# AdaLN side work in a diffusion trunk: row sums by 32x32 transposes and one full-size product, and the vectors dealt anew to the FFN halves

## The chip, the cores and the metric

One core of a Trainium2 chip runs the whole program: TensorE (PE, matmul), VectorE (DVE), ScalarE (ACT), GpSimd (POOL), and SyncE (SP), which issues the DMA transfers. The metric is the device time of one execution in microseconds; the number that counts is the median of several executions.

## What is computed

Two layers of a diffusion backbone over 256 latent tokens and 256 context tokens of width 1024. Each layer is a half-step SwiGLU feed-forward (FFN), a token mixer (windowed attention, short convolution and global attention, merged by gates), and a second half-step FFN. Each sub-layer is normalised and modulated by vectors that come from the conditioning:

```
def _ada(cvec, w, b):
    m = jax.nn.silu(cvec) @ w + b                    # (1024) @ (1024, 9*1024)
    return [m[..., j, :, :] for j in range(N_MOD)]   # 9 vectors: shift, scale, gate, three times

m, mc = _ada(c, w_ada[i], b_ada[i]), _ada(c_ctx, w_ada[i], b_ada[i])
x  = x  + 0.5 * m[2]  * _swiglu(_modulate(x,  g, m[0],  m[1]),  wg, wu, wd)
xc = xc + 0.5 * mc[2] * _swiglu(_modulate(xc, g, mc[0], mc[1]), wg, wu, wd)
...                                                  # mixer with m[3], m[4], m[5]; FFN with m[6], m[7], m[8]
```

All is float32. The conditioning is two vectors (latent and context), so each of the 18 modulation "vectors" below means 1024 values for each of the two.

## The kernel before

Activations are held transposed, features on the 128 partitions and the 512 tokens (256 of each stream) along the free dimension. Every large product is made of float32r matmuls in three parts: a weight block and an activation are each split into a high part and a remainder (`wh`, `wl` and `hh`, `hl`), and `mm_chunk` (lines 202 to 214) issues three matmuls for each block of 128 rows: high by high (line 211), high by low (212), low by high (213). A chunk is eight such blocks, 24 matmuls; in the FFN's down projection six or five, 18 or 15. `split_w` (line 185) makes `wh` by a ScalarE copy (188) and `wl` by a VectorE subtraction (189); there are three buffers of each.

Modulation vectors 0 and 1 of layer 0 are made at the start of the program by TensorE. The other 16 are made as side work within three of the four FFN halves by the class `Side`. For each vector, a step loads 128 rows of `w_ada` (a tile `adar`, 128x1024, line 267) and VectorE multiplies it by a per-partition scalar and adds it into an accumulator `adac` of 128x2x1024, once for each of the two conditionings (lines 278 and 282). After eight steps the accumulator holds, on each partition, a partial sum; the sum over the 128 partitions is still missing. `rows` (line 289) takes it on TensorE: for each conditioning v and each j of 0 to 3 a product of a 128x32 matrix `pick` (ones in column v) with 256 columns of the accumulator, written to 32 partitions of a PSUM tile. These are eight fp32 products; the trace counts two matmuls for each, and all have line 298. `ada_done` then transposes the PSUM tile by 32x32 blocks on VectorE (242), adds the bias (244) and scales (249 or 255).

Where the side work stands is set by calls: `ffn` calls `side` once ahead of each chunk pair and each half of a down projection, and calls 4 to 33 carry one or two steps each:

```
h = ffn(i, 0, h, (0, 1), side(4, 34, 1, 2) if i else side(4, 34, 2), (i, 1), ...)
```

Seven vectors (2 to 8 of layer 0) go to the first FFN half, five (0 to 4 of layer 1) to the second of layer 0, four (5 to 8 of layer 1) to the first of layer 1. From this program order a list scheduler in the build sets each engine's order; the engines run theirs in order and wait on semaphores. At the end of an FFN half the `Queue` runs the next norm's steps (`norm`, `modulate`; line 360 is the variance, 394 and 196 make the next `hl`), and the mixer's first chunks are the keys (`keys`, line 526; `keys_rstd` with lines 539 to 548).

Of the kernel before, what the change touches and what calls it, by code (L numbers as in the profile page):

```python
# [60 lines left out]
def trunk(ctx, tc, x, c, ctxt, c_ctx, w_ada, b_ada, norm_g, ffn_w_gate, ffn_w_up, ffn_w_down,  # L61
# [77 lines left out]
    ident_b = const.tile([P, P], BF16, name="ident_b")  # L139
    mask_b = const.tile([P, 2, P], BF16, name="mask_b")  # L140
    sel = const.tile([P, 32], F32, name="sel")
    pick = const.tile([P, 2, 32], F32, name="pick")
    sink_t = const.tile([P, DEPTH, NH], F32, name="sink_t")
    nsink_t = const.tile([P, DEPTH, NH], F32, name="nsink_t")

# [8 lines left out]
    def make_rest():  # L154
        vl.append(transposed_rows(*vl_rows[1], "vl1"))
        nc.vector.tensor_copy(ident_b, ident)
        nc.vector.tensor_copy(mask_b, cst[:, MSK:MSK + 2 * P].rearrange("p (a b) -> p a b", a=2))

        nc.vector.memset(sel, 0.0)
        nc.vector.tensor_copy(sel[:, 0:2], blk2)  # L160

        nc.vector.memset(pick, 0.0)
        for v in range(2):
            nc.vector.memset(pick[:, v, v:v + 1], 1.0)
        nc.vector.tensor_scalar(out=nsink_t, in0=sink_t, scalar1=-1.0, scalar2=None, op0=ALU.mult)

    def b_ada_v(i, k0, n):
# [72 lines left out]
    def ada_done(i, a, ps, k0=0, n=KD):  # L240
        tt = small.tile([P, S], F32, tag="t1k", name="ada_t", bufs=2)
        nc.vector.transpose(out=tt[:, :32 * n], in_=ps[:, :32 * n])
        m = mods[i][:, KD * a + k0:KD * a + k0 + n, :]
        nc.vector.tensor_tensor(
            out=m, in0=tt[:, :32 * n].rearrange("p (m r) -> p m r", r=32)[:, :, 0:2],
            in1=b_ada_v(i, KD * a + k0, n).unsqueeze(2).to_broadcast([P, n, 2]), op=ALU.add,
        )
        if a % 3 == 1:
            nc.vector.scalar_tensor_tensor(
                out=m, in0=m, scalar=1.0,  # L250
                in1=norm_v(i, a // 3)[:, k0:k0 + n].unsqueeze(2).to_broadcast([P, n, 2]),
                op0=ALU.add, op1=ALU.mult,
            )
        elif a in (2, 8):
            nc.vector.tensor_scalar(out=m, in0=m, scalar1=0.5, scalar2=None, op0=ALU.mult)

    class Side:
        def __init__(self):  # L260
            self.todo, self.loaded, self.acc, self.full = [], [], None, None

        def load(self, pool):
            if self.todo:
                i, a, k = self.todo.pop(0)
                raw = pool.tile([P, D], F32, tag="adar", name="adar", bufs=2)
                nc.sync.dma_start(out=raw, in_=w_ada[i][k * P:(k + 1) * P, a * D:(a + 1) * D])
                self.loaded.append((i, a, k, raw))

        def add(self, pool):  # L270
            if not self.loaded:
                return
            i, a, k, raw = self.loaded.pop(0)
            if k == 0:
                self.acc = pool.tile([P, 2, D], F32, tag="adac", name="adac", bufs=1)
            for v in range(2):
                if k == 0:
                    nc.vector.tensor_scalar(
                        out=self.acc[:, v], in0=raw, scalar1=c32[:, k, v:v + 1], scalar2=None, op0=ALU.mult
                    )  # L280
                else:
                    nc.vector.scalar_tensor_tensor(  # L282
                        out=self.acc[:, v], in0=raw, scalar=c32[:, k, v:v + 1], in1=self.acc[:, v],
                        op0=ALU.mult, op1=ALU.add,
                    )
            if k == KD - 1:
                self.full = (i, a, self.acc)

        def rows(self):
            if self.full is None:  # L290
                return
            i, a, acc_t = self.full
            self.full = None
            ps = aux()
            for v in range(2):
                r4 = acc_t[:, v].rearrange("p (m j r) -> p j m r", j=4, r=32)
                for j in range(4):
                    nc.tensor.matmul(
                        ps[32 * j:32 * j + 32, :S], pick[:, v], r4[:, j], start=(v == 0), stop=(v == 1)
                    )  # L300
            ada_done(i, a, ps)

        def step(self, pool, n):
            for _ in range(n):
                self.rows()
                self.add(pool)
                self.load(pool)

        def flush(self, pool):
            while self.loaded or self.full:  # L310
                self.rows()
                self.add(pool)

    ada_side = Side()

# [122 lines left out]
    def ffn(i, f, h, streams, side, tail, first=None):  # L438
        x = parts_of(h)
        with tc.tile_pool(name="ffn", bufs=1) as fp:  # L440
            for f0, fn in ((0, 12), (12, 10)):
                g = [fp.tile([P, 12, T], F32R, tag=t, name=t) for t in ("gh", "gl")]
                for fb in range(0, fn, 2):
                    c0 = (f0 + fb) * P
                    given = f0 + fb == 0 and first is not None
                    if not given:
                        raws = [load(w[i, f], 0, KD, c0) for w in (ffn_w_gate, ffn_w_up)]
                    ws = []
                    parts = [(cc, streams) for cc in range(2)]
                    if f0 + fb == 0 and not given:  # L450
                        ws = [split_w(raw, KD, slice(0, P)) for raw in raws]
                        if len(streams) == 2:
                            parts = [(cc, (v,)) for v in streams for cc in range(HEAD)] + parts[HEAD:]
                    for cc, st in parts:
                        queue.finish(*st)
                        side(fp)
                        ts = slice(st[0] * S, (st[-1] + 1) * S)
                        fc = fb + cc
                        ps = first[cc] if given else [acc(), acc()]
                        for p, raw in () if given else zip(ps, raws):  # L460
                            w = ws.pop(0) if ws else split_w(raw, KD, slice(cc * P, (cc + 1) * P))
                            mm_chunk(p[:, ts], w, x, 0, KD, KD, ts)
                        sg = small.tile([P, T], F32, tag="t2k", name="sg", bufs=4)
                        nc.scalar.activation(out=sg[:, ts], in_=ps[0][:, ts], func=AF.Silu)
                        nc.vector.tensor_tensor(out=sg[:, ts], in0=ps[1][:, ts], in1=sg[:, ts], op=ALU.mult)  # L465
                        split_x(g[0][:, fc, ts], g[1][:, fc, ts], sg[:, ts])
                raws_d = {}

                def down(mb, ts, f0=f0, fn=fn, g=g, raws=raws_d):
                    if mb not in raws:  # L470
                        raws[mb] = fp.tile([P, 12, WB], F32, tag="rawd", name="rawd", bufs=2)
                        nc.sync.dma_start(
                            out=raws[mb][:, :fn],
                            in_=ffn_w_down[i, f][f0 * P:(f0 + fn) * P, mb * WB:(mb + 1) * WB].rearrange(
                                "(k p) f -> p k f", p=P),
                        )
                    pm = [acc(), acc()]
                    for k0 in (0, fn // 2):
                        side(fp)
                        for e in range(2):  # L480
                            w = split_w(raws[mb][:, k0:k0 + fn // 2], fn // 2, slice(e * P, (e + 1) * P))
                            mm_chunk(pm[e][:, ts], w, parts_of(g), k0, fn // 2, fn, ts)
                    return pm

                h = project(streams, tail if f0 else None, KD // 2, down, i, 6 * f + 2)
            ada_side.flush(fp)
        return h


# [491 lines left out]
    make_rest()  # L981
    xp.close()

    ada_side.todo = [(0, a, k) for a in range(2, NMOD) for k in range(KD)]

    def side(first, end, *per):

        calls = []

        def run(pool):  # L990
            n = len(calls)
            calls.append(0)
            if first <= n < end:
                ada_side.step(pool, per[n % len(per)])
        return run

    for i in range(DEPTH):
        last = i == DEPTH - 1
        st = (0,) if last else (0, 1)
        if last:  # L1000
            assert not ada_side.todo
            ada_side.todo = [(i, a, k) for a in range(5, NMOD) for k in range(KD)]
        h = ffn(
            i, 0, h, (0, 1), side(4, 34, 1, 2) if i else side(4, 34, 2), (i, 1), None if i else first
        )
        if last:
            assert not ada_side.todo
        h = mixer(i, h, st, (i, 2))
        if not last:
            ada_start(i + 1)  # L1010
            ada_side.todo = [(i + 1, a, k) for a in range(5) for k in range(KD)]
        h = ffn(i, 1, h, st, side(4, 34, 1, 2), None if last else (i + 1, 0))


    with tc.tile_pool(name="xout", bufs=1) as op:
# [61 lines left out]
```

## Time and profile before

| | |
|---|---|
| median of 3 runs | 2099.2 us (2098.41 to 2102.4) |
| the profiled execution's own time | 2097.7 us |
| its span on the core | 2095.9 us |
| TensorE busy | 2058.8 us, 98% |
| VectorE busy | 1320.9 us, 63% |
| ScalarE busy | 850.0 us, 41% |
| GpSimd busy | 120.9 us, 6% |

The profile is of one execution. Matmuls are pipelined, so the time of one (0.39 us) is longer than the step to the next one (0.23 us); what a group of matmuls costs is better read from the starts of its neighbours. The three FFN halves with side work are the stretches of about 61 to 400, 855 to 1210 and 1210 to 1560 us.

### The profile page before, as it was taken

The numbers are of one execution on the slowest core, as the hardware profiler recorded it, in microseconds if no ns is written. First come the engines' busy times: TensorE is split into PE (matmuls) and PEld (weight loads), VectorE is DVE, ScalarE is ACT, GpSimd is POOL, SyncE is SP. The second block draws the span as 40 slices with busy tenths as digits, with TensorE's granted clock in tenths as the row PEclk, the third lists the DMA queues.
The fourth block names the chain that finished last, engine by engine and source line by source line (L and its number), as shares of the span: only waits on it lengthen the run. The fifth ranks groups of instructions, "written<-read, shape, count | busy, mean of one in ns | idle before, by whom it ended". The sixth has DMA issues, their size and how long they took to land. (4 is left out here: it accounts for less than half of the span.)

```text
span 2095.9 us, 29829 instructions
## 1 busy us (share of the span) xinstructions
PE 2058.8 (98%) x12107; PEld 1755.9 (84%) x12107; DVE 1320.9 (63%) x1984; ACT 850.0 (41%) x1347; POOL 120.9 (6%) x137
## 2 busy tenths in 40 slices
PE   6999999999999999999999999999999999999999
PEld 5888888977777888988888898888889887998998
DVE  4767877667774444676676368567435796665554
ACT  4332232546564233532223254222225677555443
POOL 0000000310000000400000020000003200011000
PEclk9999999999999999999999999999999999999999
DMA  9755655042212333454555327455330432666552
GB/s 314 233 161 188 221 182 175 26 111 57 83 50 74 92 100 125 137 191 151 173 178 159 97 81 226 131 176 168 98 102 30 133 101 89 182 198 202 176 186 75
DMA packets 247765, 295.09 MB, mean 141 GB/s; under 512 B 6708, under 2 KB 228300, under 8 KB 247628
## 3 DMA queue, kind: packets, MB, share of 16 engines
q1 hardware_dynamic: 244812, 288.91, 43.8%
q0 software_dynamic: 2560, 4.20, 1.1%
q8 instruction: 95, 1.56, 0.3%
q14 instruction: 42, 0.34, 0.1%
q10 hardware_dynamic: 256, 0.09, 0.0%
HBM read 287.93 MB, written 1.05 MB: 138 GB/s over the span
## 5 line engine op out<-in xcount | busy, mean ns | idle before, releaser
L211 PE MATMUL acc<-hh,wh 128*128 128x512 f32 (+1 forms) x2240 | 781.4, 350 | 4.1 <-ACT hh L195 2.8
L212 PE MATMUL acc<-hl,wh 128*128 128x512 f32 (+1 forms) x2240 | 778.9, 348 | 1.3 <-DVE hl L196 1.2
L213 PE MATMUL acc<-hh,wl 128*128 128x512 f32 (+1 forms) x2240 | 777.6, 348 | 0.4 <-DVE wl L189 0.4
L188 ACT ACTIVATE wh<-raw 128x1024 fp32r<-128x1024 f32 x332 | 330.5, 998 | 716.1 <-PE acc L212 570.5
L189 DVE TENSOR_TENSOR wl<-raw,wh 128x1024 fp32r<-128x1024 f32 x332 | 381.2, 1149 | 258.6 <-ACT wh L188 256.9
L211 PEld LDWEIGHTS acc<-hh,wh 128*128 128x128 f32 x2240 | 424.2, 190 | 69.2 <-issue 8.6
L212 PEld LDWEIGHTS acc<-hl,wh 128*128 128x128 f32 x2240 | 424.6, 190 | 55.8 <-DVE hl L196 2.6
L213 PEld LDWEIGHTS acc<-hh,wl 128*128 128x128 f32 x2240 | 424.5, 190 | 54.3 <-DVE wl L189 1.1
L282 DVE SCALAR_TENSOR_TENSOR adac<-adar,c,adac 128x1024 f32<-128x1024 f32 x224 | 278.6, 1279 | 27.9 <-DMA adar<-in_w_ada_dram 27.1
L213 PE MATMUL acc<-gh,wl 128*128 128x512 f32 (+1 forms) x824 | 276.4, 336 | 1.6 <-DVE wl L189 1.6
L211 PE MATMUL acc<-gh,wh 128*128 128x512 f32 (+1 forms) x824 | 277.8, 337 | 0.0
L212 PE MATMUL acc<-gl,wh 128*128 128x512 f32 (+1 forms) x824 | 276.6, 336 | 0.0
L188 ACT ACTIVATE wh<-rawd 128x640 fp32r<-128x640 f32 (+1 forms) x152 | 119.1, 783 | 313.5 <-PE acc L212 312.7
L189 DVE TENSOR_TENSOR wl<-rawd,wh 128x640 fp32r<-128x640 f32 (+1 forms) x152 | 135.0, 890 | 107.3 <-ACT wh L188 107.3
L211 PEld LDWEIGHTS acc<-gh,wh 128*128 128x128 f32 x824 | 156.4, 190 | 18.9 <-ACT wh L188 2.9
L213 PEld LDWEIGHTS acc<-gh,wl 128*128 128x128 f32 x824 | 156.2, 190 | 18.3 <-DVE wl L189 2.2
L212 PEld LDWEIGHTS acc<-gl,wh 128*128 128x128 f32 x824 | 156.4, 190 | 15.8
L465 DVE TENSOR_TENSOR sg<-acc,sg 128x512 f32<-128x512 f32 (+1 forms) x92 | 55.4, 602 | 138.3 <-PE acc L213 133.7
L332 POOL TENSOR_TENSOR ssq<-ssq,sq 128x256 f32<-128x256 f32 (+1 forms) x42 | 48.1, 1145 | 1455.2 <-ACT sq L329 1455.2
L211 PE MATMUL acc<-slot,wh 128*128 128x256 f32 (+1 forms) x352 | 113.5, 323 | 0.1
L213 PE MATMUL acc<-slot,wl 128*128 128x256 f32 (+1 forms) x352 | 113.2, 322 | 0.0
L212 PE MATMUL acc<-slot,wh 128*128 128x256 f32 (+1 forms) x352 | 113.1, 322 | 0.0
(164 smaller groups left out, 1710.1 us busy)
## 6 DMA issues: line engine op xcount, KB each, us to landing
adar<-in_w_ada_dram SPq DMA_DIRECT2D x128, 512.0 KB, 3.7
raw<-in_ffn_w_gate_dram SPq DMA_DIRECT2D x43, 1024.0 KB, 9.3
raw<-in_ffn_w_up_dram SPq DMA_DIRECT2D x43, 1024.0 KB, 5.5
rawd<-in_ffn_w_down_dram SPq DMA_DIRECT2D x16, 1536.0 KB, 6.6
raw<-in_w_gate_dram SPq DMA_DIRECT2D x24, 1024.0 KB, 5.5
rawd<-in_ffn_w_down_dram SPq DMA_DIRECT2D x16, 1280.0 KB
raw<-in_w_in_dram SPq DMA_DIRECT2D x16, 1024.0 KB, 5.4
adar<-in_w_ada_dram SPq DMA_DIRECT2D x8, 1024.0 KB, 11.9
```

The source lines that it names most:

```text
L188: nc.scalar.activation(out=wh[:, :kc], in_=raw[:, :kc, cols], func=AF.Copy)
L189: nc.vector.tensor_tensor(out=wl[:, :kc], in0=raw[:, :kc, cols], in1=wh[:, :kc].bitcast(F32), op=ALU.subtract)
L211: nc.tensor.matmul(ps, wh[:, k, :], xh, start=first, stop=False)
L212: nc.tensor.matmul(ps, wh[:, k, :], xl, start=False, stop=False)
L213: nc.tensor.matmul(ps, wl[:, k, :], xh, start=False, stop=last)
L282: nc.vector.scalar_tensor_tensor(out=self.acc[:, v], in0=raw, scalar=c32[:, k, v:v + 1], in1=self.acc[:, v], op0=ALU.mult, op1=ALU.add,)
L332: fold.tensor_tensor(out=ssq[:, ts], in0=ssq[:, ts], in1=sq, op=ALU.add)
L465: nc.vector.tensor_tensor(out=sg[:, ts], in0=ps[1][:, ts], in1=sg[:, ts], op=ALU.mult)
```

## The change

The accumulator is summed in another way. `blocks` transposes each half of the accumulator (128x512) on VectorE by 32x32 blocks and sums the runs of 32 behind it into a table `ada_r` of 128x2x32: two transposes and two sums for each conditioning. Each partition group of 32 then holds partial sums over its own 32 rows; `done` adds the four groups by one fp32 product with a 128x128 matrix `grp`, whose entry is one where two partition numbers agree modulo 32, over 64 columns. Four VectorE additions of 32 partitions each add the bias. `grp` is made in each FFN half by a sum and three copies. `pick` goes. The steps of a vector are now ten (eight adds and two `blocks`), and the vectors are dealt anew: six, five and five, with vector 8 of layer 0 in the second half and vector 4 of layer 1 in the third. A load is issued only when none is waiting, and one call earlier than the first step.

```
-        def rows(self):
...
-            ps = aux()
-            for v in range(2):
-                r4 = acc_t[:, v].rearrange("p (m j r) -> p j m r", j=4, r=32)
-                for j in range(4):
-                    nc.tensor.matmul(
-                        ps[32 * j:32 * j + 32, :S], pick[:, v], r4[:, j], start=(v == 0), stop=(v == 1)
-                    )
-            ada_done(i, a, ps)
+        def blocks(self, t, v):
+            for c0 in range(0, D, T):
+                tt = small.tile([P, T], F32, tag="t2k", name="tt", bufs=4)
+                nc.vector.transpose(out=tt, in_=t[:, v, c0:c0 + T])
+                nc.vector.tensor_reduce(
+                    out=ada_r[:, v, c0 // 32:(c0 + T) // 32], in_=tt.rearrange("p (b r) -> p b r", r=32),
+                    op=ALU.add, axis=AX.X,
+                )
+
+        def done(self, i, a, grp):
+            ps = aux()
+            nc.tensor.matmul(
+                ps[:, :64], grp.rearrange("p a r -> p (a r)"), ada_r.rearrange("p v b -> p (v b)"),
+                start=True, stop=True,
+            )
+            m = mods[i][:, KD * a:KD * (a + 1), :]
+            p4 = ps[:, :64].rearrange("p (v m j) -> p j m v", v=2, j=4)
+            for j in range(4):
+                pj = slice(32 * j, 32 * j + 32)
+                nc.vector.tensor_tensor(
+                    out=m[pj], in0=p4[pj, j],
+                    in1=b_ada_v(i, KD * a, KD)[pj].unsqueeze(2).to_broadcast([32, KD, 2]), op=ALU.add,
+                )
+            ada_scale(i, a, m)
+
+        def one(self, pool, grp):
+            if self.last is not None and not self.steps:
+                self.last(grp)
+                self.last = None
+            if self.steps:
+                self.steps.pop(0)()
+            elif self.loaded:
+                self.add(pool)
...
+            grp = fp.tile([P, 4, 32], F32, name="grp")
+            nc.vector.tensor_reduce(
+                out=grp[:, 0], in_=ident.rearrange("p (a r) -> p r a", r=32), op=ALU.add, axis=AX.X
+            )
+            for j in range(1, 4):
+                nc.vector.tensor_copy(grp[:, j], grp[:, 0])
...
-    ada_side.todo = [(0, a, k) for a in range(2, NMOD) for k in range(KD)]
+    ada_side.todo = [(0, a, k) for a in range(2, NMOD - 1) for k in range(KD)]
...
-            ada_side.todo = [(i, a, k) for a in range(5, NMOD) for k in range(KD)]
+            ada_side.todo = [(i, a, k) for a in range(4, NMOD) for k in range(KD)]
...
-            i, 0, h, (0, 1), side(4, 34, 1, 2) if i else side(4, 34, 2), (i, 1), None if i else first
+            i, 0, h, (0, 1), side(4, 34, 2, 2, 1) if i else side(4, 34, 2), (i, 1), None if i else first
...
-            ada_side.todo = [(i + 1, a, k) for a in range(5) for k in range(KD)]
-        h = ffn(i, 1, h, st, side(4, 34, 1, 2), None if last else (i + 1, 0))
+            ada_side.todo = [(i, NMOD - 1, k) for k in range(KD)]
+            ada_side.todo += [(i + 1, a, k) for a in range(4) for k in range(KD)]
+        h = ffn(i, 1, h, st, side(4, 34, 2, 2, 1), None if last else (i + 1, 0))
```

The lines of the changed kernel have other numbers: 207 to 209 are `mm_chunk`'s matmuls (211 to 213 before), 185 the `wl` (189), 192 `split_x`'s subtraction (196), 490 the `sg` product (465), 276 and 280 the adds (278 and 282), 379 the `var` (360), 413 the norm's `u` (394), 442 the update of `xT` (423).

TensorE, in the first FFN half at the first vector of the side work. Before:

```order
L211 MATMUL acc<-hh,wh 128x512
L212 MATMUL acc<-hl,wh 128x512
L213 MATMUL acc<-hh,wl 128x512
L298 MATMUL aux<-adac,pick 32x256 x8
L211 MATMUL acc<-hh,wh 128x512
```

Now:

```order
L207 MATMUL acc<-hh,wh 128x512
L208 MATMUL acc<-hl,wh 128x512
L209 MATMUL acc<-hh,wl 128x512
L300 MATMUL aux<-ada_r,grp 128x64
L207 MATMUL acc<-hh,wh 128x512
```

Eight narrow products have become one, two chunks later in the program (after 336 matmuls of `mm_chunk` instead of 288).

VectorE at the same vector. Before:

```order
L465 TENSOR_TENSOR sg<-acc,sg 128x512
L189 TENSOR_TENSOR wl<-raw,wh 128x1024
L196 TENSOR_TENSOR gl<-sg,gh 128x512
L189 TENSOR_TENSOR wl<-raw,wh 128x1024
L465 TENSOR_TENSOR sg<-acc,sg 128x512
L189 TENSOR_TENSOR wl<-raw,wh 128x1024
L196 TENSOR_TENSOR gl<-sg,gh 128x512
L242 STREAM_TRANSPOSE ada_t<-aux 128x256
L278 TENSOR_SCALAR adac<-adar,c_101 128x1024
L244 TENSOR_TENSOR mods_118<-ada_t,vl_180 128x16
```

Now:

```order
L490 TENSOR_TENSOR sg<-acc,sg 128x512
L185 TENSOR_TENSOR wl<-raw,wh 128x1024
L192 TENSOR_TENSOR gl<-sg,gh 128x512
L292 STREAM_TRANSPOSE tt<-adac 128x512 x2
L293 TENSOR_REDUCE ada_r<-tt 128x16 x2
L292 STREAM_TRANSPOSE tt<-adac 128x512 x2
L293 TENSOR_REDUCE ada_r<-tt 128x16 x2
L490 TENSOR_TENSOR sg<-acc,sg 128x512
L185 TENSOR_TENSOR wl<-raw,wh 128x1024
L192 TENSOR_TENSOR gl<-sg,gh 128x512
L276 TENSOR_SCALAR adac<-adar,c_101 128x1024 x2
```

The run of four transposes and four sums stands where a `wl` stood; that `wl` now comes behind the next `sg`.

VectorE at the end of the first FFN half, where the norm of the second stream and the mixer's first weights meet. Before:

```order
L423 SCALAR_TENSOR_TENSOR xT<-acc,mods_118,xT 128x256
L189 TENSOR_TENSOR wl<-raw,wh 128x1024
L423 SCALAR_TENSOR_TENSOR xT<-acc,mods_118,xT 128x256
L189 TENSOR_TENSOR wl<-raw,wh 128x1024 x2
L360 TENSOR_SCALAR var<-aux 128x2
L189 TENSOR_TENSOR wl<-raw,wh 128x1024
L394 TENSOR_TENSOR u<-xT,aux 128x512
```

Now:

```order
L442 SCALAR_TENSOR_TENSOR xT<-acc,mods_118,xT 128x256
L185 TENSOR_TENSOR wl<-raw,wh 128x1024
L442 SCALAR_TENSOR_TENSOR xT<-acc,mods_118,xT 128x256
L308 TENSOR_TENSOR mods_118<-aux,vl_180 32x16 x4
L185 TENSOR_TENSOR wl<-raw,wh 128x1024
L248 SCALAR_TENSOR_TENSOR mods_118<-mods_118,vl_180 128x16
L379 TENSOR_SCALAR var<-aux 128x2
L185 TENSOR_TENSOR wl<-raw,wh 128x1024
L413 TENSOR_TENSOR u<-xT,aux 128x512
```

The last vector's four additions have come here, behind the last `xT` and ahead of a `wl` and the `var`; before, that vector was done earlier, in the down projection.

## Rows read from the trace of the kernel before

**Rows 1.** The page: span, and busy time of each engine.

```profile
span 2095.9 us, 29829 instructions
...
PE 2058.8 (98%) x12107; PEld 1755.9 (84%) x12107; DVE 1320.9 (63%) x1984; ACT 850.0 (41%) x1347; POOL 120.9 (6%) x137
```

**Rows 2.** TensorE's waits: who waited for whom, us in total, times, longest.

```profile
PE aux L556 <- DVE slot L548: 2.6, 4, 1.1
...
PE acc L213 <- DVE wl L189: 2.0, 4, 0.6
```

**Rows 3.** Line 298: duration ns min/median/max, first and last start us.

```profile
L298 PE MATMUL aux<-adac,pick x256: 378/379/404, 126.8 to 1496.7; 128*32 128x256 f32 x128
```

**Rows 4.** TensorE's timeline (start us, us, what), the first vector's row sums.

```profile
125.55 0.39 PE L212 MATMUL acc<-hl,wh 128*128 128x512 f32 x1
...
126.46 0.39 PE L213 MATMUL acc<-hh,wl 128*128 128x512 f32 x1
126.78 1.07 PE L298 MATMUL aux<-adac,pick 128*32 128x256 f32 x16
...
128.59 0.40 PE L211 MATMUL acc<-hh,wh 128*128 128x512 f32 x1
```

**Rows 5.** TensorE's timeline around the last vector's row sums.

```profile
1495.65 0.39 PE L213 MATMUL acc<-hh,wl 128*128 128x512 f32 x1
...
1497.78 0.40 PE L211 MATMUL acc<-hh,wh 128*128 128x512 f32 x1
```

**Rows 6.** TensorE's timeline around two small fp32 products, 512-column neighbours.

```profile
430.83 0.40 PE L213 MATMUL acc<-hh,wl 128*128 128x512 f32 x1
431.13 0.61 PE L539 MATMUL aux<-cst,slot 128*128 128x2 f32 x4
431.59 0.48 PE L211 MATMUL acc<-hh,wh 128*128 128x512 f32 x1
...
432.37 0.40 PE L211 MATMUL acc<-hh,wh 128*128 128x512 f32 x1
```

**Rows 7.** TensorE's timeline around two fp32 products of 128 columns, 256-column neighbours.

```profile
399.83 0.28 PE L213 MATMUL acc<-gh,wl 128*128 128x256 f32 x1
399.95 0.60 PE L372 MATMUL aux<-rr,ones 128*128 128x128 f32 x4
...
400.75 0.28 PE L211 MATMUL acc<-gh,wh 128*128 128x256 f32 x1
```

**Rows 8.** VectorE's groups by shape: busy us, mean ns; idle before, releaser.

```profile
L282 DVE SCALAR_TENSOR_TENSOR adac<-adar,c,adac 128x1024 f32<-128x1024 f32 x224 | 278.6, 1279 | 27.9 <-DMA adar<-in_w_ada_dram 27.1
...
L189 DVE TENSOR_TENSOR wl<-rawd,wh 128x640 fp32r<-128x640 f32 x88 | 73.9, 842 | 60.9 <-ACT wh L188 60.9
...
L706 DVE TENSOR_REDUCE nm<-aux 128x1 f32<-128x512 f32 x64 | 41.4, 681 | 21.2 <-PE aux L698 12.1 <-PE aux L703 9.0
...
L242 DVE STREAM_TRANSPOSE ada_t<-aux 128x256 f32<-128x256 f32 x16 | 7.1, 443 | 0.0
...
L242 DVE STREAM_TRANSPOSE ada_t<-aux 128x64 f32<-128x64 f32 x8 | 1.8, 240 | 3.3 <-PE aux L235 3.3
```

**Rows 9.** Busy us by stretch: length, PE, PEld, DVE, ACT, POOL; clock, DMA share, GB/s.

```profile
61.00:400.00 339.00, 339.00 (x1648) 279.07 (x1647) 247.98 (x278) 97.08 (x129) 8.11 (x7) 1.00 0.57 183
400.00:430.00 30.00, 27.36 (x215) 25.95 (x215) 24.86 (x44) 19.56 (x36) 14.19 (x16) 1.00 0.02 7
855.00:1210.00 355.00, 353.25 (x1774) 295.58 (x1774) 226.84 (x262) 112.13 (x154) 16.21 (x16) 1.00 0.50 160
1210.00:1560.00 350.00, 348.50 (x1790) 294.44 (x1790) 211.45 (x248) 113.65 (x159) 18.68 (x18) 1.00 0.45 144
```

**Rows 10.** ScalarE's timeline, one weight split; in brackets its idle time and releaser.

```profile
121.27 1.06 ACT L188 ACTIVATE wh<-raw 128x1024 fp32r<-128x1024 f32 x1 [3.83 <-PE acc L212]
```

**Rows 11.** VectorE's timeline, a run of side work between two weight splits.

```profile
135.85 2.48 DVE L282 SCALAR_TENSOR_TENSOR adac<-adar,c,adac 128x1024 f32<-128x1024 f32 x2
...
142.08 1.22 DVE L189 TENSOR_TENSOR wl<-raw,wh 128x1024 fp32r<-128x1024 f32 x1
```

More of the change, by code (lines that the diff above doesn't have):

```diff
@@ L141, in trunk @@
     sel = const.tile([P, 32], F32, name="sel")
-    pick = const.tile([P, 2, 32], F32, name="pick")
+    ada_r = const.tile([P, 2, 32], F32, name="ada_r")
     sink_t = const.tile([P, DEPTH, NH], F32, name="sink_t")
@@ L160, in make_rest @@
         nc.vector.tensor_copy(sel[:, 0:2], blk2)
-        nc.vector.memset(pick, 0.0)
-        for v in range(2):
-            nc.vector.memset(pick[:, v, v:v + 1], 1.0)
         nc.vector.tensor_scalar(out=nsink_t, in0=sink_t, scalar1=-1.0, scalar2=None, op0=ALU.mult)
@@ L247, in ada_done, with ada_scale @@
         )
+        ada_scale(i, a, m, k0, n)
+    def ada_scale(i, a, m, k0=0, n=KD):
         if a % 3 == 1:
@@ L260, in __init__ @@
         def __init__(self):
-            self.todo, self.loaded, self.acc, self.full = [], [], None, None
+            self.todo, self.loaded, self.steps, self.last, self.acc = [], [], [], None, None
         def load(self, pool):
-            if self.todo:
+            if self.todo and not self.loaded:
                 i, a, k = self.todo.pop(0)
@@ L270, in add @@
         def add(self, pool):
-            if not self.loaded:
-                return
             i, a, k, raw = self.loaded.pop(0)
@@ L286, in add @@
             if k == KD - 1:
-                self.full = (i, a, self.acc)
-        def rows(self):
[L290 to L293, printed above, removed]
-            ps = aux()
-            for v in range(2):
-                r4 = acc_t[:, v].rearrange("p (m j r) -> p j m r", j=4, r=32)
-                for j in range(4):
-                    nc.tensor.matmul(
-                        ps[32 * j:32 * j + 32, :S], pick[:, v], r4[:, j], start=(v == 0), stop=(v == 1)
-                    )
-            ada_done(i, a, ps)
@@ L303, in step @@
-        def step(self, pool, n):
+                t = self.acc
+                self.steps = [lambda: self.blocks(t, 0), lambda: self.blocks(t, 1)]
+                self.last = lambda grp: self.done(i, a, grp)
+        def blocks(self, t, v):
[6 more added lines that the diff above has]
+                )
@@ L304, in step, with flush @@
+        def one(self, pool, grp):
[6 more added lines that the diff above has]
+                self.add(pool)
+        def step(self, pool, grp, n):
             for _ in range(n):
-                self.rows()
-                self.add(pool)
+                self.one(pool, grp)
                 self.load(pool)
[L309 to L312, printed above, removed]
+        def flush(self, pool, grp):
+            assert not self.todo
+            while self.loaded or self.steps or self.last:
+                self.one(pool, grp)
@@ L455, in ffn @@
                         queue.finish(*st)
-                        side(fp)
+                        side(fp, grp)
                         ts = slice(st[0] * S, (st[-1] + 1) * S)
@@ L478, in down @@
                     for k0 in (0, fn // 2):
-                        side(fp)
+                        side(fp, grp)
                         for e in range(2):
@@ L485, in ffn @@
                 h = project(streams, tail if f0 else None, KD // 2, down, i, 6 * f + 2)
-            ada_side.flush(fp)
+            ada_side.flush(fp, grp)
         return h
@@ L982, in trunk, with run @@
     xp.close()
-    ada_side.todo = [(0, a, k) for a in range(2, NMOD) for k in range(KD)]
+    ada_side.todo = [(0, a, k) for a in range(2, NMOD - 1) for k in range(KD)]
     def side(first, end, *per):
         calls = []
-        def run(pool):
+        def run(pool, grp):
             n = len(calls)
             calls.append(0)
+            if n == first - 1:
+                ada_side.load(pool)
             if first <= n < end:
-                ada_side.step(pool, per[n % len(per)])
+                ada_side.step(pool, grp, per[n % len(per)])
         return run
```

## The prediction

> **What bounds the kernel now.** I read the page's busy times first: TensorE is busy 2058.8 of 2095.9 us [rows 1], but a busy share is not yet a bound, so next came TensorE's own waits. The reader is to see there how little there is: VectorE's half of a split weight (`wl`, line 189) held TensorE up for 2.0 us in four waits, and the largest wait behind a VectorE result in the token mixer is 2.6 us [rows 2]. The stretch 61 to 400 us, which is most of the first feed-forward (FFN) half, has TensorE busy 339.00 of 339.00 us, while VectorE has 248 [rows 9]. So in the stretches where the adaLN side work runs, a product taken out of TensorE's queue is time taken out of the kernel, and VectorE has 27 to 40% of each stretch free. What could spoil that is lateness of VectorE: ScalarE makes a weight's `wh` the moment that TensorE has released one of three buffers [rows 10], VectorE's `wl` follows it, so `wl` has a lead of two chunks. A chunk is 24 products at 0.227 us (four take 0.91 us, from 125.55 to 126.46 [rows 4]), 5.45 us; in the down projections 18 or 15 products, 4.1 or 3.4 us.
>
> **The row sums leave TensorE.** Line 298 is in the trace with 256 matmuls of 0.379 us [rows 3], 16 for each of 16 vectors (eight fp32 products, each two passes). Their length is not their cost, since four run side by side; I take the cost from the displacement of the work around them. From the last matmul ahead (126.46) to the fourth behind (128.59) there are 2.13 us where four steps take 0.91: 1.22 us [rows 4]. The last vector gives the same 1.22 us, 1495.65 to 1497.78 [rows 5]; there are 16 of them, so 19.5 us in all.
>
> By the Trainium skill (TensorE: Matmul & The Clock Gate, Part 3: Packing small matmuls), matmuls whose outputs lie in different 32-partition column groups run concurrently, so that a set of four lasts about as long as one. By that rule alone the eight products would cost no more than two do, 0.63 us in this trace [rows 6], and the change would save only 16 × (0.63 − 0.40) = 3.7 us. The trace agrees on the concurrency (16 matmuls of 0.379 us in 1.07 us) but the displacement is 1.22 us, and that is what I use.
>
> **One full product comes.** It is fp32, 128 by 128 weights, 64 columns. The nearest rows: two fp32 products of 2 columns between 512-column matmuls (line 539) displace 432.37 − 430.83 − 0.91 = 0.63 us [rows 6], and their four passes take (431.59 − 431.13)/4 = 0.115 us each. Two of 128 columns between 256-column matmuls (line 372) displace 400.75 − 399.83 − 4 × 0.12 = 0.44 us [rows 7]. So the columns up to 128 hardly count, and one product costs at least its two passes, 0.23 us, and at most what two cost, 0.63 us. I take 0.63 less one product's passes, 0.40 us: 16 × 0.40 = 6.4 us (3.7 to 10.1). TensorE's balance is 19.5 − 6.4 = 13.1 us gained (9.4 to 15.8).
>
> **What VectorE takes over.** For each vector four transposes and four sums of 128x512. The transpose took 0.443 us at 256 columns and 0.24 at 64 [rows 8], 1.06 ns a column, so 0.714 us at 512; a 128x512 maximum (line 706) took 0.681 us. That is 4 × 0.714 + 4 × 0.681 = 5.6 us a vector, 89 us in all, and at least 78 if each hides some 0.08 us behind the next, as two of line 282 do (2.48 us together, 1.279 each [rows 8, 11]). The four adds of 32 partitions, 0.24 us each at most by the 64-column transpose, stand against a transpose of 0.443 and one add that go: nothing either way. The table of ones is made anew at each FFN half, four short operations, under 1 us.
>
> A vector's sixteen multiply-adds of line 282 and its kin cost at most 16 × 1.279 = 20 us [rows 8]. With the new dealing (6, 5 and 5 vectors to the three FFN halves that carry side work, 7, 5 and 4 before) VectorE's busy time becomes: 61 to 400 us 248 − 20 + 6 × 5.6 = 262 of 339; 855 to 1210 us 227 + 28 = 255 of 355; 1210 to 1560 us 211 + 20 + 28 = 259 of 350 [rows 9]. It stays at 72 to 77%, what the first stretch already carries. So I cost this at nothing; the cover is the two-chunk lead of `wl`. The longest run that the order now puts between two `wl` has the eight new operations, `L196` and a wait for the accumulator (second order piece): about 6.2 us. Before, there is a run of the same length, 135.85 to 142.08 us [rows 11], and TensorE doesn't wait behind it. At the first vector the order also moves one `wl` behind the run and the wait, a chunk later than it stood: of the lead of 10.9 us that leaves 10.9 − 5.45 − 1.22 = 4.2 us. In the down projection at the end of the first FFN half, where chunks are 3.4 us, the run (5.6 us) plus a `wl` of 0.84 us [rows 8] is 6.4 us against a lead of 6.8: tight, three times.
>
> The Trainium skill (VectorE: DVE Perf Modes, Rules for kernel authors) speaks against this part: it calls tensor_reduce the slowest VectorE operation and asks to restructure where it is hot. The row disagrees for this shape: 0.681 us, less than the transpose's 0.714. No row here shows one that sums runs of 32.
>
> **What moves around the mixer.** The last vector's product now stands near the end of the FFN (15 products before the second stream's norm), and its four adds, which wait for that product, stand in VectorE's queue ahead of two `wl` and the second norm's `var` (third order piece). Behind them wait the key chunks' weights. The product comes about where the adds are reached, so VectorE loses there the adds, at most 4 × 0.24 = 1 us, and a short wait; the `var` waits for TensorE anyway. From 400 to 430 us TensorE idles 2.6 us already [rows 9], so a delay can show. I put 1 us for the two such places together, with the table of ones at the entries (between 2 us gained, since the order there changes, and 6 lost). SP's queue holds the side loads in runs of up to four instead of five between weight loads, so I see no new lateness of weights.
>
> **Sum.** 13.1 − 1 = 12.1 us off the profiled execution's 2097.7 us (span 2095.9): 2085.6. The median of the runs was 2099.2, 1.5 us more, so 2087 us. Its own range is 2083 to 2092, from the ends 15.8 and 9.4 for the products and a few us at the mixer.
>
> **Rivals.**
> - VectorE becomes late (slower). Place: the `wl` behind the runs of eight. It decides once a run plus its `wl` exceeds two chunks, 6.8 us in the down projections and 10.9 elsewhere. If summing runs of 32 made the operations twice as long, a run would be 11.2 us; some seven of the 16 vectors fall into down projections, each would cost TensorE 11.2 + 0.84 − 6.8 = 5.2 us, 36 us, the other nine 11.2 + 1.2 − 10.9 = 1.5, 14 us: 2087 + 50 = 2137. To be slower than before at all needs 0.8 us a vector. For it: the tight place above. Against it: the rows of 0.443 and 0.681 us, and free VectorE time around each run.
> - The mixer entries cost more: VectorE stands behind the product while the key chunks want their weights and ScalarE's order there changes too, 3 us at each of two: 2087 + 6 = 2093, little above 2095 at worst. For it: TensorE waits there now. Against it: two chunks of lead.
> - The gain is not there, because what the eight products took is waited for anyway (2099), or they cost only what two do, 0.63 us, so that 16 × (0.63 − 0.40) = 3.7 us go (2095): 2095 to 2099. Against it: no TensorE wait in 61 to 400 us, and 1.22 us at both ends of the list.
> - The new product costs only its passes, 0.23 us, and nothing is lost at the mixer: 15.8 us, 2083.
>
> **How the numbers follow.** Forecast 0.70, VectorE late 0.06, mixer 0.10, no gain 0.07, cheaper product 0.07. The measurement can tell about 0.2%, 4 us, from no change. Faster by more (under 2095): 0.70 + 0.07 + most of the mixer case, 0.84. Within it: 0.07 and the rest of the mixer case, 0.10. Slower: 0.06. The range 2081 to 2098 leaves out the slower case and some of the case of no gain, with a little at its low end.
>
> **What would show it.** The new product with 32 matmuls and a displacement near 0.4 us; TensorE's matmul count 224 lower; transposes and sums near 0.7 us each, VectorE near 1410 us busy; TensorE's waits for `wl` still a few us; 61 to 400 us without idle TensorE. I am wrong if TensorE waits on line 189's counterpart by over 5 us, if the sums take over 1 us, or if idle TensorE between the FFN and the mixer grows by more than 3 us a place.

## The result, and the profile after

The changed kernel takes 2087.2 us (median of 6 runs, 2084.93 to 2089.88) against 2099.2 us before on the same chip (median of 5 runs, 2098.41 to 2103.1; a sixth run of 5255.81 us is left out, with it the median would be 2100.8). That is 12.0 us less; the ratio is 0.994, 95% interval 0.993 to 0.9949. The forecast was 2087. The profiled execution of the changed kernel is the slowest of its six, 2089.88 us (span 2088.1), only 7.8 us under the 2097.7 us of the profile before.

The page of the changed kernel, span and busy times:

```profile
span 2088.1 us, 29549 instructions
...
PE 2049.5 (98%) x11883; PEld 1762.6 (84%) x11883; DVE 1397.0 (67%) x2157; ACT 851.2 (41%) x1347; POOL 126.9 (6%) x137
```

Against [rows 1] there are 224 matmuls fewer, as 16 × (16 − 2) says, and VectorE has 76 us more. TensorE's waits on VectorE (who for whom, us in total, times, longest):

```profile
PE aux L581 <- DVE slot L573: 4.8, 6, 1.9
...
PE acc L209 <- DVE wl L185: 3.4, 6, 0.7
```

Both grew, from 2.6 and 2.0 us [rows 2]. The new product in TensorE's timeline (start us, us, what), at the first vector:

```profile
137.29 0.39 PE L209 MATMUL acc<-hh,wl 128*128 128x512 f32 x1
137.51 0.33 PE L300 MATMUL aux<-ada_r,grp 128*128 128x64 f32 x2
137.65 0.48 PE L207 MATMUL acc<-hh,wh 128*128 128x512 f32 x1
137.97 0.40 PE L208 MATMUL acc<-hl,wh 128*128 128x512 f32 x1
138.20 0.40 PE L209 MATMUL acc<-hh,wl 128*128 128x512 f32 x1
```

Read it as [rows 4]: from 137.29 to the third matmul behind, 0.91 us where three steps of 0.227 take 0.68. The product displaces 0.23 us; before, the eight displaced 1.22. All 16 vectors have the form of this line:

```profile
L300 PE MATMUL aux<-ada_r,grp x32: 217/248/273, 137.5 to 1608.6; 128*128 128x64 f32 x32
```

VectorE's new groups (busy us, mean ns | idle before them), and the busy times of the four stretches of [rows 9] (length, PE, PEld, DVE, ACT, POOL, then the granted clock, DMA share, GB/s):

```profile
L292 DVE STREAM_TRANSPOSE tt<-adac 128x512 f32<-128x512 f32 x64 | 42.0, 689 | 0.0
...
L293 DVE TENSOR_REDUCE ada_r<-tt 128x16 f32<-128x512 f32 x64 | 40.2, 662 | 0.1
```

```profile
61.00:400.00 339.00, 338.95 (x1607) 285.11 (x1605) 264.44 (x329) 103.19 (x141) 11.50 (x13) 1.00 0.54 171
400.00:430.00 30.00, 26.77 (x178) 25.25 (x179) 21.76 (x47) 16.89 (x31) 14.05 (x13) 0.89 0.13 36
855.00:1210.00 355.00, 353.97 (x1705) 299.86 (x1704) 251.02 (x315) 113.17 (x154) 15.38 (x16) 0.99 0.51 163
1210.00:1560.00 350.00, 348.15 (x1750) 296.90 (x1749) 254.39 (x320) 114.09 (x159) 18.24 (x17) 1.00 0.48 155
```

VectorE's work is hidden: TensorE stays busy to 400 us. The second row is the one to stop at. Idle TensorE has hardly grown there (3.2 us for 2.6), but the clock column has fallen from 1.00 to 0.89. Finer:

```profile
410.00:415.00 5.00, 3.14 (x26) 2.94 (x25) 3.12 (x6) 4.49 (x9) 2.50 (x2) 1.00 0.00 0
415.00:420.00 5.00, 5.00 (x26) 4.79 (x25) 4.45 (x11) 3.45 (x6) 4.10 (x4) 0.55 0.01 3
420.00:425.00 5.00, 5.00 (x34) 4.89 (x34) 2.90 (x7) 1.70 (x3) 0.00 (x0) 0.77 0.22 60
```

TensorE is idle for 1.86 us of the first five, and behind that it counts as busy while the granted clock is at its lower level, 1.2 GHz, for (0.45 + 0.23) × 5 / 0.5 = 6.8 us. The same happens at 872.8 and at 1620.4 us; the kernel before has none of the three. (All kernels here, before too, have the lower clock for a while in the program's first 60 us and near the end of the layer 1 mixer, at about 1873 to 1912 us.)

**Where the time went.** I compare the starts of the same products in both traces, and count how much earlier the changed kernel reaches them; a stretch's figure is what it gains (+) or gives back. "Again" is the changed kernel's second profile; the next three columns are versions that the experiments explain (e1_const, e2_early, e3_both), the one after them is f0_both. The last column is what the row sums alone should give: 1.22 us for each vector that leaves, less 0.235 for each that comes.

| stretch (times of before) | changed | again | table early | product early | both | both, again | by count |
|---|---|---|---|---|---|---|---|
| first FFN half, 61 to 397 | +7.5 | +7.5 | +7.5 | +7.3 | +7.3 | +7.3 | +7.1 |
| layer 0 mixer entry, 397 to 469 | −3.0 | −1.5 | −3.1 | +0.1 | +0.1 | +0.1 | 0 |
| second FFN half's entry, 862 to 880 | −2.4 | −1.9 | −1.5 | −2.9 | 0.0 | 0.0 | 0 |
| second half, 880 to 1233 | +5.9 | +6.5 | +5.7 | +5.8 | +5.0 | +5.0 | +4.9 |
| third half, 1254 to 1606 | +3.8 | +3.8 | +3.9 | +3.6 | +3.7 | +3.7 | +3.7 |
| layer 1 mixer entry, 1606 to 1667 | −2.9 | −0.7 | −1.9 | +0.2 | 0.0 | 0.0 | 0 |
| end of the layer 1 mixer, 1800 to 2000 | −1.0 | −1.1 | −2.2 | −0.4 | −3.4 | −1.4 | 0 |

The halves gain about what the count says; the second half's surplus in the first four columns is in part the entry's loss coming back, 0.2 to 1.0 us at about 892 us. What is short in the sum is lost at three entries, the subject of the first four runs, and in the last row, which no run was aimed at. There TensorE waits 0.3 to 1.6 us for a `slot` of ScalarE in five of the six profiles, as long as ScalarE waits just before for the transfer of a `w_o` weight; before has neither wait. The rest goes with how long the clock is low there, 6.8 us before and 6.8 or 10.2 in these. e4_deal below, without any new row, loses 5.0 us there with a wait of 2.9, so the new row sums need not be the cause, which stays open.

### The profile page after: what moved, and what is told of

Read it like the earlier page. It is cut to its first block, busy times and chain, and to the rows that moved or that the text cites. A ratio compares the mean times of both kernels' runs of the same rounds, so it can differ in the third digit from the quotient of the medians.

```text
span 2088.1 us, 29549 instructions
## 1 busy us (share of the span) xinstructions
PE 2049.5 (98%) x11883; PEld 1762.6 (84%) x11883; DVE 1397.0 (67%) x2157; ACT 851.2 (41%) x1347; POOL 126.9 (6%) x137
```

## The experiments

**The changed kernel again, and its order at the entries undone.** The kernel as it is ran once more (a0_again).

> The changed kernel as it is, beside the three below on one chip. Theory O (the order at the entries): its first profile gave back 8.7 us at three places, the two FFN-to-mixer entries (3.2 us each) and the entry of the second FFN half (2.3 us), where TensorE first waited and its granted clock then stood at 1.2 GHz for 6.8 us. If that is what the order makes, this profile shows the same three places again at about the same price, and the time is 12 to 14 us under the kernel before. Rival C (chance): the low clock fell there by chance; this profile shows it in other places or not at all, and the times scatter by 2 to 3 us for each window.

2085.2 us (2083.96 to 2090.84), ratio 0.9931 [0.9916, 0.9945]. Its profile has the same waits at the mixer entries, 1.9 and 1.8 us, but behind them only 3.4 us at the lower clock at the first and none at the second. So the wait recurs; whether the clock falls behind it, and for how long, varies.

In e1_const the table of ones is made once at the start, in columns of `cst` whose use is over, and not at each half.

```
+    grp = cst[:, MSK:MSK + P].rearrange("p (a r) -> p a r", r=32)
...
-            grp = fp.tile([P, 4, 32], F32, name="grp")
...
```

> The table of ones for the product is built once at the start, in the columns of the constants that held the attention mask before it was cast, instead of in each FFN half; nothing else. Theory O: the entry of the second FFN half is as in the kernel before (no window of 1.2 GHz at about 873 us), the mixer entries stay as they are: 2.3 us under the changed kernel. Rival C: within 1 us of the changed kernel. Rival V (VectorE's own lateness, whatever the order): under 1 us, since four short operations a half are all that goes.

2087.48 us, 0.9937 [0.9922, 0.9951]: no gain, a miss for the view that the table matters alone. The entry of the second half gives back 1.5 us instead of 2.4, the mixers 3.1 and 1.9 (3.0 and 2.9).

In e2_early the last vector's product and additions are done at call 34, in the last down projection of the half, instead of at its end: the last product of the first half is at 374 us instead of 404. (The expectation of f0_both below calls this two calls before the end of the half; there are eight to ten calls from there.)

```
+            if n == end:
+                ada_side.flush(pool, grp)
```

> The last vector's product and additions are issued at call 34, before the tail of the down projection, instead of at the end of the FFN half; the rest is the changed kernel. Theory O: both FFN-to-mixer entries are as in the kernel before (no 1.2 GHz windows at about 415 and 1620 us, ScalarE's order there is that of before), 6.4 us under the changed kernel; the entry of the second FFN half stays low. Rival C: within 1 us of the changed kernel, windows elsewhere. Rival V: the same additions and the same product have to be done, so under 1 us.

2084.57 us, 0.9924 [0.9909, 0.9939]. Both mixer entries give nothing back any more, TensorE's longest wait there is 1.1 us as before, and no lower clock follows. The entry of the second half still costs 2.9 us. Of the 6.4 us expected the median shows 0.6 against a0_again, and in time the two runs can't be told apart; the mixer's part rests on the traces. And e3_both, both edits:

> Both edits together; ScalarE's order is then that of the kernel before throughout. Theory O: the three windows are gone, 8.7 us under the changed kernel's profile, some 20 us under the kernel before (19.5 us of row sums gone, 16 products at 0.235 us = 3.8 us come, some 4 us more from side work spread differently or not). Rival C and V: within 2 us of the changed kernel, 12 to 14 us under the kernel before.

2081.78 us, 0.9917 [0.9902, 0.9931], and again, as f0_both:

> The version with both edits (ones table made once at the start, last vector's product flushed two calls before the end of the half) again, as the base of the two runs that build on it. Theory O (TensorE's waits at the entries and the 1.2 GHz stretches behind them are the whole of what is given back): 2081 to 2085 us, no stretch at 1.2 GHz between 100 and 1800 us of the span. Rival C (those stretches come and go by themselves): at least one of them near 414, 872 or 1620 us again, and a time of 2085 to 2088.

2083.53 us, 0.9927 [0.9915, 0.9939]. In both profiles no entry gives anything back, and the clock stays at 1.00 there; f0_both's at the first mixer entry:

```profile
410.00:415.00 5.00, 3.89 (x32) 3.54 (x31) 3.41 (x6) 3.91 (x10) 2.23 (x3) 1.00 0.00 0
415.00:420.00 5.00, 5.00 (x43) 4.86 (x41) 4.46 (x13) 3.74 (x7) 3.34 (x3) 1.00 0.01 2
420.00:425.00 5.00, 4.50 (x30) 3.70 (x29) 4.92 (x10) 2.48 (x6) 0.00 (x0) 1.00 0.57 161
```

This version is 18.7 and 15.6 us under before in the two calls, and e3_both is 3.4 us under the changed kernel's run beside it (a0_again). That last difference is not clear of the noise, since the two intervals overlap; that the entries are mended is shown by the traces.

**The dealing alone.** e4_deal is the kernel before, with the vectors dealt 6, 5 and 5 and the row sums on TensorE as they were.

```
...
-            ada_side.todo = [(i, a, k) for a in range(5, NMOD) for k in range(KD)]
+            ada_side.todo = [(i, a, k) for a in range(4, NMOD) for k in range(KD)]
...
```

> The kernel before with one part of the change alone: the vectors dealt 6, 5 and 5 to the three halves, the row sums left as eight small products on TensorE. Theory R (the gain is the row sums' alone): 2099 to 2103 us, as before; 12107 matmuls; TensorE's work moves between the halves by one vector's 1.22 us each way. Rival D (the dealing gives part of the gain by itself): 2090 to 2096.

2100.1 us, ratio 1.0005 [0.9996, 1.0013]: the dealing is worth nothing, the gain is the row sums'. (The new rule for the loads had no run of its own. In f0_both the halves gain what the products alone should give to 0.2 us or less, so little is left for it.) Its profile has 3.4 us of lower clock at the entry of the second half and loses 1.3 us there, without any of the new rows.

**VectorE's cover.** f1_twice is the version with both edits, each transpose and sum done twice.

```
...
+                for _ in range(2):
+                    nc.vector.transpose(out=tt, in_=t[:, v, c0:c0 + T])
...
```

> The version with both edits, with each transpose and each sum of runs of 32 done twice, the second on top of the first: about 85 us more of VectorE, its busy time from about 1400 to 1485 us, a run of 11.2 us between two wl. Theory H (VectorE's part is hidden with room to spare): 2082 to 2086, no wait of TensorE on wl over a few us. Rival V (the two-chunk lead of wl is what hides it, and 5.6 us is near its limit): runs of 11.2 us overrun the lead, 5.2 us each in seven down projections and 1.5 us each elsewhere: about 50 us, 2132, with as much more waiting on wl.

2098.84 us, ratio 1.0002 [0.9993, 1.0011]: 15.3 us more than f0_both, between the two theories, and all of the gain gone. TensorE's waits on `wl` are 8.8 us in 18 (1.9 in 4), and one of them is the rival of the prediction at work, in the first down projection. VectorE's timeline has eight transposes, seven sums and four updates of `xT` between two `wl`, and TensorE's the price:

```profile
211.93 1.82 DVE L191 TENSOR_TENSOR wl<-rawd,wh 128x768 fp32r<-128x768 f32 x2
213.67 1.30 DVE L299 STREAM_TRANSPOSE tt<-adac 128x512 f32<-128x512 f32 x2
...
224.16 0.92 DVE L191 TENSOR_TENSOR wl<-rawd,wh 128x768 fp32r<-128x768 f32 x1
```

```profile
225.13 0.80 PE L215 MATMUL acc<-gh,wl 128*128 128x512 f32 x1 [3.04 <-DVE wl L191]
```

10.5 us between the two `wl`, 3.04 us of waiting, and behind it 6.8 us at 1.2 GHz, which lose another 3.4. These, the other waits on `wl` (3.9 more than in f0_both), one of 0.9 us of the product for `ada_r`, and 1.5 at the second half's entry make 12.7 us. The profiled execution, of 2102.76 us, is 19.2 us above that of f0_both; I have no row for the rest.

**The product's price.** f2_more adds 120 products, each alone between weight products.

```
...
+            if self.some:
+                nc.tensor.matmul(
+                    aux()[:, :64], grp.rearrange("p a r -> p (a r)"), ada_r.rearrange("p v b -> p (v b)"),
...
```

> The version with both edits, with one more full-size fp32 product (same operands, output not used) ahead of each multiply-add step from the second vector on: 120 more products, each alone between weight products. Theory P (a product costs its two passes alone, 0.235 us): 120 x 0.235 = 28 us more, 2110. Rival S (a change to an fp32 product and back has a price of its own, 0.40 us in all as I predicted): 48 us more, 2130; at the upper bound of 0.63 us 76 us more, 2158.

2111.95 us, 28.4 over f0_both: 0.237 us for each, which is its two passes (0.23 by [rows 6]) and nothing for the change to an fp32 product and back.

**What makes TensorE wait at the mixer.** The chain there is: VectorE makes `vark` of the keys' squares, GpSimd raises it to a power, VectorE copies it to a slot, TensorE takes that. VectorE's timeline of the changed kernel at the layer 0 entry, then GpSimd's, then TensorE's:

```profile
407.62 0.16 DVE L379 TENSOR_SCALAR var<-aux 128x2 f32<-128x2 f32 x1 [0.33 <-PE aux L400]
407.70 1.22 DVE L185 TENSOR_TENSOR wl<-raw,wh 128x1024 fp32r<-128x1024 f32 x1
...
411.54 0.16 DVE L568 TENSOR_SCALAR vark<-aux 128x4 f32<-128x4 f32 x1
411.82 1.46 DVE L185 TENSOR_TENSOR wl<-raw,wh 128x1024 fp32r<-128x1024 f32 x1
414.19 0.29 DVE L573 COPY slot<-vark 128x256 f32<-128x256 f32 x1 [0.90 <-POOL vark L571]
```

```profile
407.86 1.62 POOL L382 TENSOR_TENSOR var<-var,expo 128x2 f32<-128x2 f32 x1 [0.31 <-DVE var L379]
...
412.18 1.98 POOL L571 TENSOR_TENSOR vark<-vark,expo 128x4 f32<-128x4 f32 x1
```

```profile
414.54 0.71 PE L581 MATMUL aux<-cst,slot 128*128 128x128 f32 x4 [1.86 <-DVE slot L573]
```

The same operations before, `vark` on VectorE, then GpSimd, then TensorE:

```profile
419.42 0.16 DVE L543 TENSOR_SCALAR vark<-aux 128x4 f32<-128x4 f32 x1
```

```profile
415.79 0.71 POOL L363 TENSOR_TENSOR var<-var,expo 128x2 f32<-128x2 f32 x1 [0.59 <-DVE var L360]
...
420.00 1.01 POOL L546 TENSOR_TENSOR vark<-vark,expo 128x4 f32<-128x4 f32 x1
```

```profile
421.39 0.71 PE L556 MATMUL aux<-cst,slot 128*128 128x128 f32 x4 [1.07 <-DVE slot L548]
```

Both powers take 0.9 to 1.0 us longer now, and each has a `wl` of VectorE beside it that began before it. Each ends about 0.57 us (two columns) or 0.87 (four) after that `wl`: 408.92 + 0.57 = 409.49 and 413.28 + 0.87 = 414.15. From the start of `vark` to that of its power there are 0.64 us now and 0.58 before, so what TensorE waits longer for is the power, not VectorE's or ScalarE's work ahead of it. Other pairs fit: in f0_both a power beside an operation with an operand in PSUM takes its 1.01 us and one behind a `hl` that began first 1.43; in the changed kernel one beside a `hl` that began after it takes 1.01.

By the Trainium skill (SBUF — State Buffer, Who interferes with whom), a VectorE instruction with two SBUF inputs contends with a GpSimd instruction that reads SBUF, for a shared port pair that is an exclusive lock, and the order of issue decides which of them waits. The rows agree where VectorE is first: `wl` has both inputs in SBUF, and the power ends 0.57 or 0.87 us behind it. Where GpSimd is first they are mixed: the `wl` at 411.82 takes 1.46 us instead of 1.22, beside GpSimd's `u` that runs from 411.65 to 412.21, but in g2_two below a `wl` that begins at 408.13, while the power lasts until 408.78, takes its usual 1.22.

Two runs put more VectorE work at the first key chunk of f0_both: two additions with both inputs in SBUF (g2_two), or two transposes with one (g3_one), in the same places of VectorE's order. The added results are not used.

```
...
+                if (b, v) == (0, 0):
+                    dm = tmp()
+                    for _ in range(2):
+                        nc.vector.tensor_tensor(out=dm, in0=xT[:, 0], in1=xT[:, 1], op=ALU.add)
...
```

> The version with both edits, and at the first key chunk of each mixer two more VectorE additions of 128x512 with both inputs in SBUF (0.69 us each, output not used). By the program's order one of them stands behind the norm's var, and the wl of a later weight slips behind the first vark, where the changed kernel has it too. Theory L (a GpSimd power, which reads SBUF, doesn't run beside a VectorE operation with two SBUF inputs that began before it): the power of var at the two mixer entries 1.0 to 2.2 us (0.71 in the version with both edits), the power of the first vark 1.9 to 2.0 (1.01), TensorE's longest wait for the normed keys' slot 1.9 to 2.1 us (1.1), a stretch at 1.2 GHz behind it at least at one of the two entries, 1 to 3 us each: 2084 to 2089. Rival T (VectorE's own lateness is all): powers 0.71 and 1.01 as before, no stretch at 1.2 GHz, 2082 to 2084.

> As the run with two additions, but with two transposes of 128x512 (0.69 us each, one SBUF input) in their place, in the same places of VectorE's order. Theory L: the power of var back at about 0.71 us, since only the transpose stands beside it (up to 1.3 if the wl behind it begins first), and the power of the first vark 1.9 to 2.0 us, since the wl still stands beside that; TensorE's longest wait for the slot 1.9 to 2.1 us, and a time of 2083 to 2088. Rival T: the same as with the additions, powers 0.71 and 1.01, 2082 to 2084.

2087.43 us, 0.9945 [0.9931, 0.9959], and 2087.39 us, 0.9947 [0.9935, 0.996]. VectorE's timeline beside the power of `var`, of g2_two and then of g3_one:

```profile
407.54 0.68 DVE L575 TENSOR_TENSOR tmp<-xT 128x512 f32<-128x512 f32 x1
408.13 1.22 DVE L191 TENSOR_TENSOR wl<-raw,wh 128x1024 fp32r<-128x1024 f32 x1
```

```profile
407.56 0.70 DVE L575 STREAM_TRANSPOSE tmp<-xT 128x512 f32<-128x512 f32 x1
```

GpSimd's timeline of g2_two, then of g3_one, then of f0_both:

```profile
407.70 1.08 POOL L388 TENSOR_TENSOR var<-var,expo 128x2 f32<-128x2 f32 x1 [0.32 <-DVE var L385]
...
411.26 1.55 POOL L424 TENSOR_SCALAR u<-u,mods 128x256 f32<-128x256 f32 x1 [2.48 <-DVE vark L568]
412.78 1.00 POOL L571 TENSOR_TENSOR vark<-vark,expo 128x4 f32<-128x4 f32 x1
```

```profile
407.73 0.71 POOL L388 TENSOR_TENSOR var<-var,expo 128x2 f32<-128x2 f32 x1 [0.31 <-DVE var L385]
...
411.29 1.55 POOL L424 TENSOR_SCALAR u<-u,mods 128x256 f32<-128x256 f32 x1 [2.86 <-DVE vark L568]
```

```profile
408.89 0.71 POOL L388 TENSOR_TENSOR var<-var,expo 128x2 f32<-128x2 f32 x1 [0.58 <-DVE var L385]
412.60 0.56 POOL L424 TENSOR_SCALAR u<-u,mods 128x256 f32<-128x256 f32 x1 [3.00 <-DVE u L419]
413.13 1.01 POOL L571 TENSOR_TENSOR vark<-vark,expo 128x4 f32<-128x4 f32 x1
```

The power of `var` is 1.08 us beside the addition and 0.71 beside the transpose: VectorE's being busy is not enough, the second SBUF input makes the difference. It is not the only thing that does: in f0_both the multiply `adac<-adar,c`, with one SBUF tensor (128x1024 in 0.73 us), has a power of `var` beside it that takes 1.29 us (at 1240.57). At `vark` my expectation missed the instruction: the `wl` that slipped behind it held up GpSimd's `u` (1.55 us for 0.56), and the power behind that began late instead of lasting long. What follows is as expected, in both runs: TensorE's longest wait for the slot is 1.9 us,

```profile
PE aux L585 <- DVE slot L577: 4.9, 6, 1.9
```

where f0_both has

```profile
PE aux L581 <- DVE slot L573: 2.7, 4, 1.1
```

Behind it the clock falls at both mixer entries, for 3.4 or 6.8 us. The two mixer entries give back 2.7 and 1.6 us in g2_two's trace, 1.4 and 2.8 in g3_one's, where f0_both gives back nothing. So 2.7 us of VectorE work in the wrong place cost about 4 us. The medians say the same (11.1 us under before in both runs, f0_both 15.6), but they are of two calls and their intervals overlap.

## Why the prediction was right, point by point

- **Row sums leave TensorE, 19.5 us.** Right. In f0_both the three halves gain 7.3, 5.0 and 3.7 us; 1.22 us for each vector gone and 0.235 for each new product make 7.1, 4.9 and 3.7. By the packing rule of the Trainium skill (TensorE: Matmul & The Clock Gate, Part 3: Packing small matmuls) alone the eight would have cost 0.63 us, and the seven, five and four of them that went could not have given this much.
- **One full product, 0.40 us each, 6.4 in all.** Mis-sized: 0.235 in the timeline, 0.237 by f2_more, 3.8 us in all, the lower bound. I had split the 0.63 us of two products [rows 6] into one product's passes and a fixed rest of 0.17; a 64-column product between two 512-column ones shows no such rest. The balance was 15.8 and not 13.1 us.
- **VectorE's new work at nothing.** Right: 0.689 and 0.662 us (forecast 0.714 and 0.681), 1397 us busy (1410), and 264, 251 and 254 us in the three stretches (262, 255, 259). The rule of the Trainium skill that calls tensor_reduce the slowest VectorE operation (VectorE: DVE Perf Modes, Rules for kernel authors) doesn't hold for this shape: the sum took less than the transpose. But the cover is thin, as the prediction feared: in f1_twice twice the work undoes the gain. The price of the rival was too high (36 + 14 us for runs of 11.2 us; the run gave 15.3), because one run overran its lead by as much as 3 us, where I had put 5.2 us on seven, and all waits on `wl` came to 8.8 us.
- **The mixer entries at 1 us together.** The step that failed. In the profile they give back 5.9 us at the two mixers and 2.4 at the second half's entry, in a0_again 2.2 and 1.9. I had priced VectorE's loss (the additions and a short wait) and not what moves: the `wl` that the additions push back now stands beside a GpSimd power on the path, TensorE's wait goes from 1.1 to 1.9 us, and the clock may fall behind it. The rival of 3 us a place had the size, but named VectorE's standing behind the product and ScalarE's order, not GpSimd or the clock. (The 2.6 us that the prediction calls the largest wait there is the sum of four, the longest 1.1 [rows 2].) The sign that I named, idle TensorE growing by over 3 us a place, never came, since time at 1.2 GHz counts as busy.
- **The sum.** 12.1 us forecast; 12.0 and 15.3 us measured in two calls. Two errors partly cancelled: the products gained 2.7 us more than I gave them, and the entries took 3 to 7 us more. That the forecast came within 0.2 us of the median is therefore luck; a few us was what the sum was good for. With the entries mended the 15.8 us of the balance stand, within the intervals of both calls: 18.7 and 15.6.

Open: the entry of the second FFN half. Its clock fell in the changed kernel, in a0_again, e1_const, e2_early, e4_deal, f1_twice and g3_one, and not in before, e3_both, f0_both, f2_more or g2_two. e1_const and g3_one have the same two waits there as f0_both and g2_two, 1.1 us for `ssq` and 0.2 for `hl`, and e4_deal has none of the new operations. So I can't tie the 1.3 to 2.9 us there to one edit.

## What to carry to other kernels

When an edit moves work to an engine with room, look at what its new instructions push aside: an operation with two SBUF inputs that slips beside a short GpSimd step on the path can double that step. Read the clock column beside the busy times, since a stretch at the lower clock looks fully busy. Price a product that stands alone by its passes, not by a share of a pair.

## What was not expected of the hardware

A GpSimd power of two columns took 0.71 us beside a 32x32-block transpose of 0.70 us, which has one SBUF input, 1.08 beside a 0.69 us addition and 1.62 beside a 1.22 us `wl`, the last two with two SBUF inputs. TensorE's clock fell to 1.2 GHz for 3.4 or 6.8 us behind waits of 1.8 to 2.0 us at a mixer entry in nine of ten cases (changed kernel, again, e1_const, g2_two and g3_one, two entries each), and in none of the 14 where the longest wait was 1.1 us or less (the other seven kernels). At the second half's entry it fell in some kernels behind no more than 1.1 us. One 128x128 fp32 product of 64 columns displaced 0.235 us of the work around it, eight with 32 output partitions each displaced 1.22 together.
